# Stick-breaking scores of a head pair: three 64-row matmuls per head on the two halves of the array's rows, in place of two 128-row ones on stacked hi and lo

## The chip, the cores and the metric

The kernel runs on one core of a Trainium2 chip. The metric is the device time of one execution in microseconds (us). The engines are called by the names of the profile: PE is TensorE (matmuls), PEld its weight loads, DVE VectorE, ACT ScalarE, POOL GpSimd, and SP SyncE, whose queue issues nearly all DMAs here.

## What is computed

One decoder layer on a sequence of 1024 tokens of width 1024, in float32: an RMSNorm, one wide input projection, three mixers (an mLSTM, a short convolution, stick-breaking attention), their output projections under sigmoid gates, an MLP and a last RMSNorm. The change concerns the scores `z` of the stick-breaking attention, which has 16 heads of width 64:

```python
def stick_breaking(q, k, v):                      # [1, 1024, 16, 64]
    qf = q.astype(f32) * (d ** -0.5)
    ...
        mask = key_pos[None, :] < q_pos[:, None]
        z = jnp.einsum('bhqd,bshd->bhqs', qblk, kf)
        log_beta = jax.nn.log_sigmoid(z)
        log_1m = jnp.where(mask, log_beta - z, 0.0)
        cum = jnp.cumsum(log_1m, axis=-1)
        log_a = log_beta + cum[..., -1:] - cum
        a = jnp.where(mask, jnp.exp(log_a), 0.0)
        return jnp.einsum('bhqs,bshd->bqhd', a, vf)
```

## The kernel before

**Precision.** Every float32 operand of a matmul is split into a hi part, rounded to the matmul's `fp32r` format, and a lo part, the rest. A product is made of three matmuls, hi x hi, hi x lo and lo x hi, which sum in one PSUM bank (`mm3`, L129 to L132). `split` (L134) makes the parts: ACT copies the hi (L136), DVE subtracts (L137).

**Stages.** The program goes through the mLSTM heads, then the stick-breaking heads, then the three output projections, the output projection and the MLP. The stick-breaking stage lies between 515 and 1245 us. It goes through eight pairs of heads `p`. For each pair, `sb_v` (for every second pair) and `sb_qk` project V, K and Q; `sb_attn` computes the attention; `sc_unit(p)` computes one eighth of the convolution mixer. The projections are dense matmuls of 128 rows and 512 columns (or 256 for V), on lines 130 to 132.

**Scores.** A head has 64 channels and the array 128 rows. `sb_qk` therefore stacks for each head hi and lo: the tile of Q holds its hi in one half of the partitions and its lo in the other; the two tiles of K, `kx` and `ky`, hold (hi, lo) and (lo, hi). The two matmuls of L556 and L557 give (Q hi x K hi + Q lo x K lo) and (Q hi x K lo + Q lo x K hi). To put the hi and lo of K into the other half, `ev_k` sends four DMAs (L530 to L533) per 512 tokens.

**Attention.** `sb_attn` goes through four groups `G` of 256 queries, from the last to the first, then the two heads `hh`, then the two blocks `ti` of 128 queries, then the chunks `ch` of at most 512 keys. For each chunk: two score matmuls into a bank `z` (there are two such banks), two sigmoids on ACT into tiles `u` and `be` (L559, L560), on POOL the mask of the diagonal (L564, L566) or a column handed on (L570), a product scan on DVE (L572), a multiplication on POOL (L573). When a head's four or fewer `be` tiles of the group are done, PE transposes them (L590), ACT and DVE split them, and PE multiplies by V (L603 to L607). There are six `u` and ten `be` tiles.

**Order.** The order of each engine's instructions is set at build time by a scheduler. `sb_attn` is written under `high_priority(offset=AHEAD)`, so that its instructions come first where the scheduler finds them ready; the dense matmuls of the convolution and of the next pair fill the rest of PE's queue. On the chip each queue goes in its fixed order.

Of the kernel before, what the change touches and what calls it, by code (L numbers as in the profile page):

```python
# [11 lines left out]
AF = mybir.ActivationFunctionType  # L12
ALU = mybir.AluOpType
# [3 lines left out]
P = 128  # L17
# [11 lines left out]
C_SBQ, C_SBK, C_SBV = 7176, 8200, 9224  # L29
# [9 lines left out]
def hybrid_block_kernel(  # L39
# [18 lines left out]
    nc = tc.nc  # L58
# [31 lines left out]
    def free(*ts):  # L90
        for t in ts:
            owner[id(t)].free.append(t)
# [13 lines left out]
    def g(name):  # L106
        return rings[name].get()

    def plan(base, **counts):
        for n, c in counts.items():  # L110
            rings[n] = base.carve(n, c)
# [12 lines left out]
    def f32(ap):  # L124
        return ap.bitcast(F32)

    mm = nc.tensor.matmul
# [31 lines left out]
    def dense_ws(w, c0, rhs, evac):  # L159
        parts = load_w(w, 0, KO, c0, P, 4)  # L160
        for th in range(2):
            ps = g("acc")
            for ko in range(KO):
                rh, rl = rhs[ko][th]
                wh, wl = parts[ko // 4]
                ks = slice((ko % 4) * P, (ko % 4 + 1) * P)
                mm3(ps, wh[:, ks], wl[:, ks], rh[:, :512], rl[:, :512], ko == 0, ko == KO - 1)
            evac(th, ps)
            free(ps)
        for p in parts:  # L170
            free(*p)
# [334 lines left out]
        return vt  # L506

    def sb_qk(p):
        Q = [[None, None], [None, None]]
        T = [[None, None] for _ in range(4)]  # L510

        def ev_q(th, ps):
            a, b = g("Q"), g("Q")
            A, B = slice(0, 64), slice(64, 128)
            r = slice(0, 512)
            nc.scalar.activation(a[A, r], ps[A, :], AF.Copy)
            nc.scalar.activation(b[B, r], ps[B, :], AF.Copy)
            nc.vector.tensor_tensor(a[B, r], ps[A, :], f32(a[A, r]), ALU.subtract)
            nc.vector.tensor_tensor(b[A, r], ps[B, :], f32(b[B, r]), ALU.subtract)
            Q[0][th], Q[1][th] = a, b  # L520

        def ev_k(th, ps):
            t1, t2, t3, t4 = [g("T") for i in range(4)]
            A, B = slice(0, 64), slice(64, 128)
            r = slice(0, 512)
            nc.scalar.activation(t1[A, r], ps[A, :], AF.Copy)
            nc.scalar.activation(t2[B, r], ps[B, :], AF.Copy)
            nc.vector.tensor_tensor(t3[A, r], ps[A, :], f32(t1[A, r]), ALU.subtract)
            nc.vector.tensor_tensor(t4[B, r], ps[B, :], f32(t2[B, r]), ALU.subtract)
            nc.sync.dma_start(f32(t1[B, r]), f32(t3[A, r]))  # L530
            nc.sync.dma_start(f32(t3[B, r]), f32(t1[A, r]))
            nc.sync.dma_start(f32(t2[A, r]), f32(t4[B, r]))
            nc.sync.dma_start(f32(t4[A, r]), f32(t2[B, r]))  # L533
            for i, t in enumerate((t1, t2, t3, t4)):
                T[i][th] = t

        dense_ws(w_in, C_SBK + p * P, hT, ev_k)
        dense_ws(w_in, C_SBQ + p * P, hT, ev_q)
        return Q, T

    def sb_attn(p, Q, T, vt):
        for G in range(3, -1, -1):
            yo = g("yo")
            for hh in range(2):
                kx, ky = (T[0], T[2]) if hh == 0 else (T[1], T[3])
                ga = {}
                for ti in (1, 0):
                    Tt = 2 * G + ti
                    qs = Q[hh][Tt // 4][:, (Tt % 4) * P:(Tt % 4 + 1) * P]
                    n = (Tt + 1) * P  # L550
                    nch = (n + 511) // 512
                    prev = None
                    for ch in range(nch - 1, -1, -1):
                        w = min(512, n - ch * 512)
                        ps = g("z")
                        mm(ps[:, :w], qs, kx[ch][:, :w], start=True, stop=False)  # L556
                        mm(ps[:, :w], qs, ky[ch][:, :w], start=False, stop=True)  # L557
                        u, be = g("u"), g("be")
                        nc.scalar.activation(u[:, :w], ps[:, :w], AF.Sigmoid, scale=-0.125)  # L559
                        nc.scalar.activation(be[:, :w], ps[:, :w], AF.Sigmoid, scale=0.125)  # L560
                        free(ps)
                        if prev is None:
                            dg = slice(w - P, w)
                            nc.gpsimd.affine_select(out=u[:, dg], in_=u[:, dg], compare_op=ALU.is_gt, fill=1.0,  # L564
                                                    base=0, pattern=[[-1, P]], channel_multiplier=1)
                            nc.gpsimd.affine_select(out=be[:, dg], in_=be[:, dg], compare_op=ALU.is_gt, fill=0.0,  # L566
                                                    base=0, pattern=[[-1, P]], channel_multiplier=1)
                            nc.gpsimd.memset(u[:, w:w + 1], 1.0)
                        else:
                            nc.gpsimd.tensor_copy(u[:, w:w + 1], prev[:, 0:1])  # L570
                        ur = u[:, 0:w][:, ::-1]
                        nc.vector.tensor_tensor_scan(ur, ur, ur, u[:, w:w + 1], ALU.mult, ALU.bypass)  # L572
                        nc.gpsimd.tensor_tensor(be[:, :w], be[:, :w], u[:, 1:w + 1], ALU.mult)  # L573
                        if prev is not None:
                            free(prev)
                        prev = u
                        ga[ti, ch] = be
                    free(prev)
                pav = g("av")
                ns = 2 * G + 2  # L580
                last = 1 if G else 0
                for s2 in range(G, -1, -1):
                    pt = g("tp")
                    for k in (0, 1):
                        s = 2 * s2 + k
                        for ti in (0, 1):
                            if s == ns - 1 and ti == 0:
                                continue
                            blk = ga[ti, s // 4][:, (s % 4) * P:(s % 4 + 1) * P]
                            nc.tensor.transpose(pt[:, k * 256 + ti * P:k * 256 + (ti + 1) * P], blk, ident)  # L590
                    ah, al = g("ah"), g("ah")
                    if s2 == G:
                        split(ah[:, 0:256], al[:, 0:256], pt[:, 0:256])
                        split(ah[:, 256:384], ah[:, 384:512], pt[:, 384:512])
                    else:
                        split(ah[:, 0:512], al[:, 0:512], pt)
                    free(pt)
                    for k in ((1, 0) if s2 == G else (0, 1)):
                        s = 2 * s2 + k
                        hd = 2 * (p % 2) + hh  # L600
                        vs = vt[s][:, hd * P:(hd + 1) * P]
                        if s == ns - 1:
                            mm(pav[:, 256:512], vs, ah[:, 256:512], start=True, stop=True)  # L603
                            continue
                        o = slice(k * 256, (k + 1) * 256)
                        mm(pav[:, 0:256], vs, ah[:, o], start=(s == ns - 2), stop=False)  # L606
                        mm(pav[:, 0:256], vs, al[:, o], start=False, stop=(s == last))  # L607
                    free(ah, al)
                free(*ga.values())
                tmp = g("avt")  # L610
                hi_r = slice(0, 64) if hh == 0 else slice(64, 128)
                lo_r = slice(64, 128) if hh == 0 else slice(0, 64)
                nc.scalar.activation(tmp[hi_r, 0:512], pav[lo_r, :], AF.Copy)
                nc.vector.tensor_tensor(yo[hi_r, 0:512], pav[hi_r, :], tmp[hi_r, 0:512], ALU.add)
                free(pav, tmp)
            for o in (256, 384):
                nc.vector.tensor_tensor(yo[:, 128:256], yo[:, 128:256], yo[:, o:o + P], ALU.add)
            nc.sync.dma_start(ysb_d[p][:, G * 256:(G + 1) * 256], yo[:, 0:256])
            free(yo)
            if G == 2:  # L620
                free(*[t[1] for t in Q + T])
        free(*[t[0] for t in Q + T])


    def sc_unit(ct):
# [55 lines left out]
            ml_attn(h, st)  # L681
    unplan(ring_r, "q", "k", "v", "ph", "ks", "C")
    unplan(ring_f, "e", "k32", "nmb", "C32", "ft")
    plan(ring_r, Q=6, T=10, V=8, ah=8)
    plan(ring_f, u=6, be=10, yo=2, avt=1)
    vt = None
    for p in range(8):
# [216 lines left out]
    for u in range(FF // 256):  # L904
# [3 lines left out]
        s = {}  # L908
# [130 lines left out]
```

## Time and profile before

| | us |
|---|---|
| median of 3 runs | 2571.91 (2571.35 to 2572.49) |
| the profiled execution | 2567.67 |
| its span, first to last instruction | 2566.0 |
| PE busy in the span | 2510.3 (98%) |
| DVE, ACT, POOL busy | 1323.2, 1036.1, 490.8 |
| PE busy in the stick-breaking stage, 515 to 1245 | 726.57 of 730 |

Times in the rows are counted from the start of the span. A row of the timeline has the start, the duration, the engine, the line, and the operation with its tiles and sizes. `128*128` is the shape of the array's tile that a matmul uses (rows*columns), `128x512` the rows and columns of what it streams. Matmuls are pipelined: a row's duration reaches from its start to its end, and the next row can start earlier. A group of instructions has its count, its busy time in us, the mean duration of one in ns, and the idle time of the engine before them with what ended it.

### The profile page before, as it was taken

Reading aid. Unit: us, or ns where it says so; the run is one execution under the profiler, and the core shown is the slowest. Engines: PE = TensorE matmul, PEld = TensorE weight load, DVE = VectorE, ACT = ScalarE, POOL = GpSimd, SP = SyncE. Lnnn points to the kernel's source line nnn. Section 1 sums busy time; section 2 is a strip of 40 time slices with the busy share of each in tenths; the row PEclk is TensorE's granted clock in tenths of the full one; section 3 lists DMA queues with packets and bytes.
Section 4 is the critical chain, followed back from the end, with each engine's and each line's share of the span. In section 5 each row is a group of like instructions: output and inputs, shape, how many; then the busy total and the mean of one; then the engine's idle time right before and its main releaser. Section 6 shows DMA issues by size and latency. Waiting matters only on the chain.

```text
span 2566.0 us, 34552 instructions
## 1 busy us (share of the span) xinstructions
PE 2510.3 (98%) x12984; PEld 2121.0 (83%) x12984; DVE 1323.2 (52%) x2189; ACT 1036.1 (40%) x2138; POOL 490.8 (19%) x928
## 2 busy tenths in 40 slices
PE   7999999999999999999999999999979999999997
PEld 6899898988888888888888888888858888788886
DVE  6465463767677677577522223224364334444435
ACT  6343333455455455455512212124455555522211
POOL 3000010044344254254100000000263222000000
PEclk9999999999999999999999999999989999999998
DMA  4121111222211221222312313213233334522203
GB/s 121 46 70 46 54 42 54 58 59 58 67 48 51 68 59 44 71 56 60 104 45 74 91 50 99 58 54 123 86 106 109 107 111 139 184 90 83 99 29 111
DMA packets 218560, 197.90 MB, mean 77 GB/s; under 512 B 16400, under 2 KB 176144, under 8 KB 218392
## 3 DMA queue, kind: packets, MB, share of 16 engines
q1 hardware_dynamic: 215944, 191.23, 24.3%
q10 hardware_dynamic: 2448, 4.46, 0.5%
q8 instruction: 102, 1.67, 0.3%
q14 instruction: 66, 0.54, 0.1%
HBM read 149.49 MB, written 37.77 MB: 73 GB/s over the span
## 4 chain that ended last, share of the span: by engine, by line
PE 93%; DVE 3%; DMA 1%; POOL 1%; ACT 1%; issue 1%; SPq 0%; DVEq 0%; POOLq 0%; ACTq 0%
PE ps L130 28%; PE ps L131 28%; PE ps L132 28%; PE ps L590 2%; PE ps L557 1%; PE ps L556 1%; PE ps L607 1%; PE ps L606 1%; DVE gr L137 1%; DVE gf L572 0%; DMA wr<-in_w_in_dram 0%; POOL gf L573 0%; DMA wl<-gd 0%; DMA wr<-in_w_down_dram 0%; DVE gf L1010 0%
## 5 line engine op out<-in xcount | busy, mean ns | idle before, releaser
L132 PE MATMUL ps<-gr,wl 128*128 128x512 f32 x1872 | 740.9, 396 | 2.6 <-DVE wl L137 2.6
L130 PE MATMUL ps<-gr,wh 128*128 128x512 f32 x1856 | 734.6, 396 | 0.0
L131 PE MATMUL ps<-gr,wh 128*128 128x512 f32 x1856 | 734.1, 396 | 0.0
L132 PEld LDWEIGHTS ps<-gr,wl 128*128 128x128 f32 x1872 | 352.1, 188 | 83.9 <-DVE wl L137 3.3
L130 PEld LDWEIGHTS ps<-gr,wh 128*128 128x128 f32 x1856 | 348.9, 188 | 78.7
L131 PEld LDWEIGHTS ps<-gr,wh 128*128 128x128 f32 x1856 | 348.6, 188 | 78.9
L136 ACT ACTIVATE wh<-wr 128x512 fp32r<-128x512 f32 (+1 forms) x268 | 167.7, 631 | 445.7 <-PE ps L131 386.7
L137 DVE TENSOR_TENSOR wl<-wr,wh 128x512 fp32r<-128x512 f32 (+1 forms) x258 | 183.4, 718 | 295.4 <-ACT wh L136 291.0
L132 PE MATMUL ps<-gr,gr 128*128 128x512 f32 (+3 forms) x900 | 330.0, 368 | 1.4 <-DVE gr L137 1.4
L131 PE MATMUL ps<-gr,gr 128*128 128x512 f32 (+3 forms) x900 | 330.7, 369 | 0.0
L130 PE MATMUL ps<-gr,gr 128*128 128x512 f32 (+3 forms) x900 | 327.0, 367 | 1.0 <-ACT gr L136 1.0
L572 DVE TENSOR_TENSOR_SCAN gf<-gf 128x512 f32<-128x512 f32 (+1 forms) x192 | 200.9, 1048 | 100.4 <-POOL gf L564 56.8
L130 PE MATMUL ps<-wh,gr 128*128 128x256 f32 (+2 forms) x800 | 231.1, 290 | 2.6 <-ACT gr L139 2.6
L132 PE MATMUL ps<-wh,gr 128*128 128x256 f32 (+2 forms) x800 | 227.9, 288 | 0.2 <-DVE gr L140 0.2
L131 PE MATMUL ps<-wl,gr 128*128 128x256 f32 (+2 forms) x788 | 224.2, 285 | 0.0
L573 POOL TENSOR_TENSOR gf<-gf,gf 128x512 f32<-128x512 f32 (+1 forms) x192 | 185.3, 967 | 175.8 <-DVE gf L572 144.8
L759 POOL TENSOR_TENSOR gf<-gf,gf 128x512 f32<-128x512 f32 x48 | 68.2, 1426 | 704.5 <-ACT gf L853 575.7
L136 ACT ACTIVATE gr<-ps 128x256 fp32r<-128x256 f32 (+2 forms) x304 | 129.7, 442 | 170.7 <-PE ps L132 70.7
L130 PEld LDWEIGHTS ps<-gr,gr 128*128 128x128 f32 x900 | 169.1, 188 | 32.4 <-ACT gr L136 1.5
L132 PEld LDWEIGHTS ps<-gr,gr 128*128 128x128 f32 x900 | 169.5, 188 | 31.8 <-DVE gr L137 1.9
L131 PEld LDWEIGHTS ps<-gr,gr 128*128 128x128 f32 x900 | 169.4, 188 | 30.2
L137 DVE TENSOR_TENSOR gr<-ps,gr 128x256 fp32r<-128x256 f32 (+2 forms) x304 | 142.7, 483 | 59.1 <-ACT gr L136 56.0
(204 smaller groups left out, 3406.7 us busy)
## 6 DMA issues: line engine op xcount, KB each, us to landing
wr<-in_w_in_dram SPq DMA_DIRECT2D x102, 512.0 KB, 3.7
gd<-gf SPq DMA_DIRECT2D x64, 256.0 KB, 2.7
wr<-in_w_down_dram SPq DMA_DIRECT2D x32, 512.0 KB, 4.0
gr<-gd SPq DMA_DIRECT2D x52, 256.0 KB, 2.8
gf<-in_w_up_dram SPq DMA_DIRECT2D x40, 256.0 KB, 3.0
gr<-gr SPq DMA_DIRECT2D x64, 128.0 KB, 2.2
gf<-in_x_dram SPq DMA_DIRECT2D x31, 256.0 KB, 3.0
wr<-in_w_up_dram SPq DMA_DIRECT2D x24, 256.0 KB, 2.9
```

The costliest lines, as they stand in the source:

```text
L130: mm(ps, lh, rh, start=start, stop=False, skip_group_check=chain)
L131: mm(ps, lh, rl, start=False, stop=False, skip_group_check=chain)
L132: mm(ps, ll, rh, start=False, stop=stop, skip_group_check=chain)
L136: nc.scalar.activation(hi, src, AF.Copy)
L137: nc.vector.tensor_tensor(lo, src, f32(hi), ALU.subtract)
L556: mm(ps[:, :w], qs, kx[ch][:, :w], start=True, stop=False)
L557: mm(ps[:, :w], qs, ky[ch][:, :w], start=False, stop=True)
L572: nc.vector.tensor_tensor_scan(ur, ur, ur, u[:, w:w + 1], ALU.mult, ALU.bypass)
L573: nc.gpsimd.tensor_tensor(be[:, :w], be[:, :w], u[:, 1:w + 1], ALU.mult)
L590: nc.tensor.transpose(pt[:, k * 256 + ti * P:k * 256 + (ti + 1) * P], blk, ident)
L606: mm(pav[:, 0:256], vs, ah[:, o], start=(s == ns - 2), stop=False)
L759: nc.gpsimd.tensor_tensor(dst[:, :512], a[:, :512], b[:, :512], op)
```

## The change

`sb_qk` splits K and Q like every other operand: for 512 tokens one tile with the hi and one with the lo of both heads, head 0 in partitions 0 to 63 and head 1 in 64 to 127. The four DMAs per K eviction fall away. `sb_attn` takes both heads in one pass: for each block and chunk it gets two banks and issues hi x hi, hi x lo and lo x hi, each for head 0 on the upper half of the array's rows and head 1 on the lower half. Then follow the same sigmoids, masks, scans and multiplications for either head. `ga` and `prev` exist for each head; the transposes and the products with V come after both heads' scores of a group. The six Q and ten T tiles become eight and eight.

```diff
     def sb_qk(p):
-        Q = [[None, None], [None, None]]
-        T = [[None, None] for _ in range(4)]
...
-        def ev_k(th, ps):
-            t1, t2, t3, t4 = [g("T") for i in range(4)]
-            A, B = slice(0, 64), slice(64, 128)
-            r = slice(0, 512)
-            nc.scalar.activation(t1[A, r], ps[A, :], AF.Copy)
-            nc.scalar.activation(t2[B, r], ps[B, :], AF.Copy)
-            nc.vector.tensor_tensor(t3[A, r], ps[A, :], f32(t1[A, r]), ALU.subtract)
-            nc.vector.tensor_tensor(t4[B, r], ps[B, :], f32(t2[B, r]), ALU.subtract)
-            nc.sync.dma_start(f32(t1[B, r]), f32(t3[A, r]))
-            nc.sync.dma_start(f32(t3[B, r]), f32(t1[A, r]))
-            nc.sync.dma_start(f32(t2[A, r]), f32(t4[B, r]))
-            nc.sync.dma_start(f32(t4[A, r]), f32(t2[B, r]))
...
+        Q, T = [None, None], [None, None]
+
+        def ev(side, name):
+            def f(th, ps):
+                hi, lo = g(name), g(name)
+                split(hi[:, :512], lo[:, :512], ps)
+                side[th] = (hi, lo)
+            return f
...
     def sb_attn(p, Q, T, vt):
         for G in range(3, -1, -1):
             yo = g("yo")
-            for hh in range(2):
-                kx, ky = (T[0], T[2]) if hh == 0 else (T[1], T[3])
-                ga = {}
-                for ti in (1, 0):
...
-                        ps = g("z")
-                        mm(ps[:, :w], qs, kx[ch][:, :w], start=True, stop=False)
-                        mm(ps[:, :w], qs, ky[ch][:, :w], start=False, stop=True)
...
+            ga = [{}, {}]
+            for ti in (1, 0):
...
+                    pss = [g("z"), g("z")]
+                    qh, ql = Q[Tt // 4]
+                    kh, kl = T[ch]
+                    for m, (l, r) in enumerate(((qh, kh), (qh, kl), (ql, kh))):
+                        for hh in range(2):
+                            hs = slice(hh * 64, hh * 64 + 64)
+                            mm(pss[hh][:, :w], l[hs, qs], r[hs, :w], start=m == 0, stop=m == 2)
+                    for hh in range(2):
+                        ps = pss[hh]
                         u, be = g("u"), g("be")
...
+            for hh in range(2):
                 pav = g("av")
...
-    plan(ring_r, Q=6, T=10, V=8, ah=8)
+    plan(ring_r, Q=8, T=8, V=8, ah=8)
```

The scheduler sets the order anew. In the rows that follow, `ps_166` and `ps_167` are the two score banks (after the change, of head 0 and of head 1), `gr_95` to `gr_110` tiles of Q and K, and lines 130 to 132 dense matmuls; the streamed operand stands first, the loaded one second.

PE, the first scores of the first pair and the second scores after them. Before:

```order
L556 MATMUL ps_166<-gr_105,gr_97 128x512
L557 MATMUL ps_166<-gr_107,gr_97 128x512
L556 MATMUL ps_167<-gr_101,gr_97 128x512
L557 MATMUL ps_167<-gr_103,gr_97 128x512
L130 MATMUL ps_165<-gr_65,wh_154 128x512
```

The same place after the change:

```order
L541 MATMUL ps_166<-gr_105,gr_97 128x512
L541 MATMUL ps_167<-gr_105,gr_97 128x512
L541 MATMUL ps_166<-gr_106,gr_97 128x512
L541 MATMUL ps_167<-gr_106,gr_97 128x512
L541 MATMUL ps_166<-gr_105,gr_98 128x512
L541 MATMUL ps_167<-gr_105,gr_98 128x512
L130 MATMUL ps_165<-gr_65,wh_154 128x512
```

Here the two heads alternate. PE again, after the change, the next two chunks, some 20 dense matmuls further on:

```order
L131 MATMUL ps_165<-gr_94,wh_155 128x512
L541 MATMUL ps_166<-gr_103,gr_97 128x512
L541 MATMUL ps_166<-gr_104,gr_97 128x512
L541 MATMUL ps_166<-gr_103,gr_98 128x512
L132 MATMUL ps_165<-gr_93,wl_160 128x512
L130 MATMUL ps_164<-gr_63,wh_156 128x512
L541 MATMUL ps_167<-gr_103,gr_97 128x512
L541 MATMUL ps_167<-gr_104,gr_97 128x512
L541 MATMUL ps_167<-gr_103,gr_98 128x512
L131 MATMUL ps_164<-gr_64,wh_156 128x512
```

Here the scheduler has put each head's three together, with dense matmuls between the heads. Of the 576 score matmuls after the change, most stand as in this second piece; the score matmuls form 185 unbroken runs, where there were 188 before.

## Rows read from the trace of the kernel before

**Rows 1.** The page: busy us (share of the span) and instructions of each engine.

```profile
PE 2510.3 (98%) x12984; PEld 2121.0 (83%) x12984; DVE 1323.2 (52%) x2189; ACT 1036.1 (40%) x2138; POOL 490.8 (19%) x928
```

**Rows 2.** Busy us by stretch (PE, PEld, DVE, ACT, POOL, granted clock), and the stage's sum.

```profile
515.00:606.00 91.00, 91.00 (x468) 76.66 (x467) 64.37 (x93) 49.19 (x104) 39.13 (x82) 1.00 0.23 62
...
sum 730.00, PE 726.57 PEld 625.41 DVE 518.73 ACT 393.51 POOL 309.94; mean PE 90.82 PEld 78.18 DVE 64.84 ACT 49.19 POOL 38.74
```

**Rows 3.** What PE waited for, 515 to 1245 us: us, times, longest us.

```profile
PE ps L607 <- DVE gr L137: 2.9, 3, 1.0
PE ps L603 <- DVE gr L137: 0.2, 1, 0.2
```

**Rows 4.** Timeline, matmuls and weight loads: start us, us, what.

```profile
527.62 0.39 PE L131 MATMUL ps<-gr,wh 128*128 128x512 f32 x1
...
529.48 0.39 PE L556 MATMUL ps<-gr,gr 128*128 128x512 f32 x1
529.48 0.19 PEld L557 LDWEIGHTS ps<-gr,gr 128*128 128x128 f32 x1
...
529.71 0.40 PE L557 MATMUL ps<-gr,gr 128*128 128x512 f32 x1
...
535.54 0.40 PE L131 MATMUL ps<-gr,wh 128*128 128x512 f32 x1
```

**Rows 5.** The two score lines: count, ns min/median/max, first and last start, forms.

```profile
L556 PE MATMUL ps<-gr,gr x192: 218/388/483, 529.5 to 1232.1; 128*128 128x512 f32 x96, 128*128 128x384 f32 x32, 128*128 128x256 f32 x32, 128*128 128x128 f32 x32
L557 PE MATMUL ps<-gr,gr x192: 270/389/486, 529.7 to 1232.2; 128*128 128x512 f32 x96, 128*128 128x384 f32 x32, 128*128 128x256 f32 x32, 128*128 128x128 f32 x32
```

**Rows 6.** Timeline of PE: score matmuls of 384, 256 and 128 columns.

```profile
535.78 0.34 PE L556 MATMUL ps<-gr,gr 128*128 128x384 f32 x1
535.95 0.34 PE L557 MATMUL ps<-gr,gr 128*128 128x384 f32 x1
536.13 0.39 PE L132 MATMUL ps<-gr,wl 128*128 128x512 f32 x1
...
659.79 0.28 PE L556 MATMUL ps<-gr,gr 128*128 128x256 f32 x1
659.91 0.28 PE L557 MATMUL ps<-gr,gr 128*128 128x256 f32 x1
660.02 0.28 PE L130 MATMUL ps<-wh,gr 128*128 128x256 f32 x1
...
662.16 0.22 PE L556 MATMUL ps<-gr,gr 128*128 128x128 f32 x1
662.22 0.27 PE L557 MATMUL ps<-gr,gr 128*128 128x128 f32 x1
662.33 0.33 PE L132 MATMUL ps<-wh,gr 128*128 128x256 f32 x1
662.50 0.28 PE L130 MATMUL ps<-wh,gr 128*128 128x256 f32 x1
```

**Rows 7.** DMA issues: count, KB each, median us from issue to landing.

```profile
gr<-gr SPq DMA_DIRECT2D x64, 128.0 KB, 2.2
```

**Rows 8.** Groups by line: a half's copy on ACT, a half's subtraction on DVE.

```profile
L517 ACT ACTIVATE gr<-ps 64x512 fp32r<-64x512 f32 x16 | 9.5, 593 | 0.2
...
L529 DVE TENSOR_TENSOR gr<-ps,gr 64x512 fp32r<-64x512 f32 x15 | 10.4, 695 | 1.9 <-PE ps L556 1.6
```

**Rows 9.** Timeline of PE: two gate transposes with another tile shape among 264-column matmuls.

```profile
28.45 0.28 PE L131 MATMUL ps<-wl,gr 128*128 128x264 f32 x1
28.57 0.27 PE L282 MATMUL ps<-ident,gcol 128*4 128x128 f32 x1
28.68 0.27 PE L283 MATMUL ps<-ident,gcol 128*4 128x128 f32 x1
28.70 0.37 PE L130 MATMUL ps<-wh,gr 128*128 128x264 f32 x1
28.91 0.29 PE L131 MATMUL ps<-wl,gr 128*128 128x264 f32 x1
```

More of the change, by code (lines that the diff above doesn't have):

```diff
@@ L508, in sb_qk @@
     def sb_qk(p):
-        Q = [[None, None], [None, None]]
-        T = [[None, None] for _ in range(4)]
-        def ev_q(th, ps):
-            a, b = g("Q"), g("Q")
-            A, B = slice(0, 64), slice(64, 128)
-            r = slice(0, 512)
[L516 to L520, printed above, removed]
-        def ev_k(th, ps):
-            t1, t2, t3, t4 = [g("T") for i in range(4)]
-            A, B = slice(0, 64), slice(64, 128)
-            r = slice(0, 512)
-            nc.scalar.activation(t1[A, r], ps[A, :], AF.Copy)
-            nc.scalar.activation(t2[B, r], ps[B, :], AF.Copy)
-            nc.vector.tensor_tensor(t3[A, r], ps[A, :], f32(t1[A, r]), ALU.subtract)
-            nc.vector.tensor_tensor(t4[B, r], ps[B, :], f32(t2[B, r]), ALU.subtract)
-            nc.sync.dma_start(f32(t1[B, r]), f32(t3[A, r]))
-            nc.sync.dma_start(f32(t3[B, r]), f32(t1[A, r]))
-            nc.sync.dma_start(f32(t2[A, r]), f32(t4[B, r]))
-            nc.sync.dma_start(f32(t4[A, r]), f32(t2[B, r]))
[L534 to L538, printed above, removed]
+        Q, T = [None, None], [None, None]
[5 more added lines that the diff above has]
+            return f
+        dense_ws(w_in, C_SBK + p * P, hT, ev(T, "T"))
+        dense_ws(w_in, C_SBQ + p * P, hT, ev(Q, "Q"))
         return Q, T
@@ L543, in sb_attn @@
             yo = g("yo")
-            for hh in range(2):
-                kx, ky = (T[0], T[2]) if hh == 0 else (T[1], T[3])
-                ga = {}
-                for ti in (1, 0):
[L548 to L554, printed above, removed]
-                        ps = g("z")
-                        mm(ps[:, :w], qs, kx[ch][:, :w], start=True, stop=False)
-                        mm(ps[:, :w], qs, ky[ch][:, :w], start=False, stop=True)
+            ga = [{}, {}]
+            for ti in (1, 0):
+                Tt = 2 * G + ti
+                qs = slice((Tt % 4) * P, (Tt % 4 + 1) * P)
+                n = (Tt + 1) * P
+                nch = (n + 511) // 512
+                prev = [None, None]
+                for ch in range(nch - 1, -1, -1):
+                    w = min(512, n - ch * 512)
+                    pss = [g("z"), g("z")]
[7 more added lines that the diff above has]
+                        ps = pss[hh]
                         u, be = g("u"), g("be")
@@ L561, in sb_attn @@
                         free(ps)
-                        if prev is None:
+                        if prev[hh] is None:
                             dg = slice(w - P, w)
@@ L569, in sb_attn @@
                         else:
-                            nc.gpsimd.tensor_copy(u[:, w:w + 1], prev[:, 0:1])
+                            nc.gpsimd.tensor_copy(u[:, w:w + 1], prev[hh][:, 0:1])
                         ur = u[:, 0:w][:, ::-1]
@@ L573, in sb_attn @@
                         nc.gpsimd.tensor_tensor(be[:, :w], be[:, :w], u[:, 1:w + 1], ALU.mult)
[L574 to L578, printed above, removed]
+                        if prev[hh] is not None:
+                            free(prev[hh])
+                        prev[hh] = u
+                        ga[hh][ti, ch] = be
+                free(*prev)
+            for hh in range(2):
                 pav = g("av")
@@ L588, in sb_attn @@
                                 continue
-                            blk = ga[ti, s // 4][:, (s % 4) * P:(s % 4 + 1) * P]
+                            blk = ga[hh][ti, s // 4][:, (s % 4) * P:(s % 4 + 1) * P]
                             nc.tensor.transpose(pt[:, k * 256 + ti * P:k * 256 + (ti + 1) * P], blk, ident)
@@ L608, in sb_attn @@
                     free(ah, al)
-                free(*ga.values())
+                free(*ga[hh].values())
                 tmp = g("avt")
@@ L620, in sb_attn @@
             if G == 2:
-                free(*[t[1] for t in Q + T])
-        free(*[t[0] for t in Q + T])
+                free(*Q[1], *T[1])
+        free(*Q[0], *T[0])
     def sc_unit(ct):
```

## The prediction

> **What bounds the kernel now.** I read the page's busy table first, then busy time by stretch, then what TensorE waits for, then the matmuls one by one. The profiled execution took 2567.67 us, 1.65 of them outside its span, and TensorE is busy for 98% of that span [rows 1]. An average says little about one stage, so the next view is the attention stage alone, from 515 to 1245 us, cut into eight stretches of about one head pair: TensorE is busy 726.57 of 730 us there, at a granted clock of 1.00, the upper of the two levels (2.4 GHz) [rows 2]. The next engine, DVE, has 518.73. What TensorE waited for in the stage adds up to 3.1 us, nearly all of it three waits for a split on DVE [rows 3]. As busy matmuls overlap in this trace, busy time alone could mislead; the starts settle it. From 527.62 to 535.78 there are 35 matmuls of 512 columns, one each 8.16 / 35 = 0.233 us, score matmuls (L556, L557) among dense ones without a hole [rows 4]. So TensorE's queue is the path in this stage, and it has filler: whenever attention is not ready, dense matmuls of the next projections stand in the queue. A matmul more in this queue costs its spacing, one fewer gives it back, and what happens on other engines counts only if TensorE comes to wait for it.
>
> **The scores: what they cost now.** There are 96, 32, 32 and 32 matmuls of 512, 384, 256 and 128 columns on each of the two lines [rows 5]. Their price is the distance to the next start, not their duration of 0.39 us. It is 0.233 us for 512 columns [rows 4], 0.175 for 384 (535.78, 535.95, 536.13), 0.117 for 256 (659.79, 659.91, 660.02), and for 128 columns 0.11: L556 (662.16), L557 and a 256-column matmul take until the next start at 662.50, and 0.34 - 0.117 leaves 0.22 for the two [rows 6]. Hence 192 x 0.233 + 64 x 0.175 + 64 x 0.117 + 64 x 0.11 = 44.7 + 11.2 + 7.5 + 7.0 = 70.4 us.
>
> **What is added.** Three matmuls of the same width and the same 128 loaded columns stand where two stood: 576 for 384. If a 64-row matmul takes its turn like a 128-row one, the scores cost 70.4 x 1.5 = 105.6 us, which is **+35.2 us**. The number of columns streamed sets the spacing, and half of the rows lying idle doesn't shorten it: in rows 4 and 6 the spacing follows the columns (0.233 and 0.117 for 512 and 256).
>
> **What can be given back.** Two matmuls on opposite halves may run side by side, but only where they are neighbours in TensorE's queue. The diff writes six matmuls alternating between the heads; the built order does not keep that. Of its 185 unbroken runs of score matmuls, 127 are three of one head, 26 one or two of one head, and only 32 hold both: at 512 columns 8 runs of six, 4 of five, 4 of four and 4 of two, all alternating; four alternating runs of six at 128 columns; and eight in which one head's matmul merely abuts the other's. No row of this trace shows two matmuls side by side, so the price has two ends. One end is nothing. The other is full overlap, in which the alternating 512-column runs save 8 x 3 + 4 x 2 + 4 x 2 + 4 x 1 = 44 spacings of 0.233, 10.3 us, and the others at most 4 x 3 x 0.11 + 4 x 0.117 + 4 x 0.11 = 2.2: 12.5 us in all. Between them lies the weight load. Each matmul has its own; it starts as the matmul before it starts [rows 4], and 128-column matmuls, which leave nothing but the load to wait for, come no closer than 0.11 us [rows 6]. With starts 0.11 apart and 0.233 on the same half, an alternating six ends after 0.809 us instead of 1.398 and saves 0.589; five save 0.466, four 0.356, two 0.123; 128-column runs save nothing, and the four pairs of 384 and 256 columns 0.065 each. That is 4.7 + 1.9 + 1.4 + 0.5 + 0.3 = **-8.8 us**. I take this value, because a load and a matmul do run beside one another in rows 4 and the halves have separate weights and banks, while nothing there shows two loads at once. Added and given back: +35.2 - 8.8 = **+26.4 us**.
>
> The Trainium skill bears on this on its page TensorE: Matmul & The Clock Gate, Part 3, Packing small matmuls: matmuls that target different row groups run concurrently, about 4 ns apart at their starts, and only matmuls that follow each other do, since they start and end in program order. By its figure the sum would be the full-overlap end, an estimate of +22.7; no row here shows it.
>
> **What is removed and moved.** Each K eviction loses four SBUF-to-SBUF DMAs, 64 in all of 128 KB and 2.2 us [rows 7], and each K or Q eviction becomes one 128-partition ACT and one DVE instruction in place of two of 64 partitions (some 593 and 695 ns each [rows 8]). On ACT and DVE that is 32 instructions fewer, some 19 us each. All of it is costed at nothing, because TensorE hardly waits: no score matmul waited for a K copy, dense matmuls stood ahead of it, and rows 3 name no DMA. The gain can't exceed the stage's waits of 3.1 us. The SP queue only loses work; its weight loads move up and were not late. The loops now hold both heads' weights of a group: up to 8 of the 10 `be` tiles instead of 4, and both score banks at once. Where a group then has to wait for the group before, dense matmuls stand behind it in the same queue and wait too. The built order puts such matmuls ahead (23 dense ones between the first two score runs), so I put nothing in the sum, from -3.1 to the bound of the third rival.
>
> **The switch of tile shape** is the large unknown. Now 185 runs of 64-row matmuls lie between 128-row ones: 370 switches. The nearest rows are the gate transposes, which use a tile of 128 rows and few columns, among 264-column matmuls: the switch in comes 0.12 us after a 264-column start, as any other; the second transpose and the 264-column matmul behind it take from 28.68 to 28.91, 0.23, which is just 0.11 + 0.12 [rows 9]. Nothing was lost. The other bound is that the array empties first: a matmul lasts 0.39 us [rows 4] and the next starts after 0.23, so 0.16 would be exposed, 370 x 0.16 = 59 us. I take zero, since rows 9 are an actual change of shape; they split columns and not rows, so the other end stays in the range.
>
> **The rivals.**
> 1. The halves don't run side by side (the change doesn't do what its loop says): +35.2, **2607 us**. For it: no pair is seen beside another in the trace. Against it: load and matmul already are.
> 2. Every switch empties the array: +26.4 + 59 = **2657 us**, and 2608 to 2657 for a part of it. Against it: rows 9. The Trainium skill speaks for it on its page TensorEngine Tiling (Array Packing), Key Properties: changing the tiling mode drains the engine. The trace doesn't agree for the column tile of rows 9, and says nothing of a row tile.
> 3. A new wait: the 32 groups (8 pairs of 4) each hold up the queue for the longest wait seen now, 1.0 us [rows 3]: +26.4 + 32 = **2630 us**. Against it: the filler.
> 4. Faster. TensorE lets the second head's three matmuls pass over the dense ones between and run beside the first head's: then 576 matmuls cost as 288, 52.8 us, -17.6, **2554 us**. It decides from 35.2 / 0.233 = 151 side-by-side 512-column pairs on; the order has 44 as neighbours. For it: weight loads run ahead of matmuls. Against it: the matmuls of rows 4 and 6 start in program order.
>
> **How the numbers follow.** The sum is a difference, so it is added to the median of 2571.91, which lies 4.2 us above the profiled execution: 2571.9 + 26.4 = **2598 us**. The forecast has 0.38 (its own range 2591 to 2604, from full overlap and the waits gone to half the overlap); rival 1 has 0.19, rival 2 0.25, rival 3 0.06, rival 4 0.06, and 0.06 goes to a mixture that ends within 0.2%, 5 us, which is about what a measurement of this kernel can tell from no change. The range 2588 to 2640 leaves out rival 4, the no-change case and the upper third of rival 2, 0.08: 2 in 10. Faster 0.06, same 0.06, slower 0.88.
>
> **What would show it.** In the profile after, 576 score matmuls with a tile of 64 rows; the stage some 26 us longer, at the same busy share; where A B A B stand in a row, starts 0.11 and 0.12 apart by turns; where three of one head stand, 0.233. Starts 0.233 apart in the alternating runs mean rival 1; an extra gap before and behind each run rival 2; named waits of TensorE for ACT, DVE or POOL in the stage rival 3. A stage that isn't longer would prove the forecast wrong outright.

## The result, and the profile after

The changed kernel takes 2660.89 us (median of 5 runs, 2658.59 to 2661.34) against 2572.49 us before: 88.4 us more, a ratio of 1.034 (95% interval 1.0324 to 1.0355). The forecast was 2598 with a range up to 2640; rival 2 stood at 2657.

The page's first lines after, busy time and instructions, answer to [rows 1]:

```profile
span 2659.2 us, 34649 instructions
PE 2602.5 (98%) x13176; PEld 2132.0 (80%) x13176; DVE 1317.9 (50%) x2157; ACT 1020.2 (38%) x2106; POOL 509.5 (19%) x928
```

TensorE's share is 98% as before, and its 93 us more of span are 92 us more of busy time. Busy time by stretch, the stage now being some 89 us longer, and what PE waited for in it (to [rows 2, 3]):

```profile
515.00:1334.00 819.00, 817.67 (x4241) 636.14 (x4240) 511.87 (x761) 378.01 (x834) 331.50 (x651) 1.00 0.14 41
...
PE ps L590 <- DVE gr L137: 1.3, 3, 0.4
```

No new wait is named, the granted clock is 1.00, and PE counts as busy for 817.67 of 819 us. Read by its busy share this stage looks perfect. Yet the matmuls don't explain it: 192 more cost 35.2 us at most, and 89 came. The time is inside what counts as busy, between the starts. Here is the timeline at the first scores of the first pair, matmuls (PE) and weight loads (PEld), and at the next scores after them:

```profile
528.87 0.19 PEld L132 LDWEIGHTS ps<-gr,wl 128*128 128x128 f32 x1
529.10 0.40 PE L132 MATMUL ps<-gr,wl 128*128 128x512 f32 x1
529.42 0.53 PEld L541 LDWEIGHTS ps<-gr,gr 64*128 64x128 f32 x6 [0.36 <-issue]
529.42 0.96 PE L541 MATMUL ps<-gr,gr 64*128 64x512 f32 x6
...
530.31 0.19 PEld L130 LDWEIGHTS ps<-gr,wh 128*128 128x128 f32 x1 [0.36 <-issue]
530.32 0.50 PE L130 MATMUL ps<-gr,wh 128*128 128x512 f32 x1
530.42 0.19 PEld L131 LDWEIGHTS ps<-gr,wh 128*128 128x128 f32 x1
530.65 0.40 PE L131 MATMUL ps<-gr,wh 128*128 128x512 f32 x1
...
535.56 0.40 PE L131 MATMUL ps<-gr,wh 128*128 128x512 f32 x1
535.88 0.53 PEld L541 LDWEIGHTS ps<-gr,gr 64*128 64x128 f32 x3 [0.37 <-issue]
535.89 0.96 PE L541 MATMUL ps<-gr,gr 64*128 64x512 f32 x3
...
536.77 0.50 PE L132 MATMUL ps<-gr,wl 128*128 128x512 f32 x1
...
537.11 0.40 PE L130 MATMUL ps<-gr,wh 128*128 128x512 f32 x1
```

Two things are to be seen. First, **six alternating matmuls take the time of three of one head**: 0.90 us from 529.42 to the next start at 530.32, and 0.88 from 535.89 to 536.77. Their loads also took the same 0.53. The halves do run side by side, loads and all. Second, **a price at each switch**. In [rows 4] the load for the next matmul starts together with the matmul before it. Here it doesn't: the last dense matmul starts at 529.10, the first 64-row load at 529.42, 0.32 later, which is 0.09 after the 0.233 that the columns take. Only then the load runs, which takes 0.11 (from 530.31, one load, to 530.42, the next), and as far as the rows show no column flows meanwhile: the matmul that starts with the load (530.32) lasts 0.50 in place of 0.40, and the next one starts 0.33 after it in place of 0.233. The loads' row has the gap as 0.36 us of idle time ended by `issue`, which means that nothing the profile can name was waited for. On the way into the 64-row tile and on the way back the same happens. From 529.10 to 530.65 it takes 1.55 us; a dense matmul, three steps of pairs and another dense one are 5 x 0.233 = 1.165. The rest is 0.385 us for two switches, **0.19 us each**. From 535.56 to 537.11 the numbers are the same.

Over all 185 runs, from where the columns before have ended to where the load behind is done, the starts add up to 164.8 us; with the pairs side by side the matmuls alone would take 105.6 - 12.5 = 93.1. That leaves 71.7 us for 370 switches, 0.194 each, whatever the columns before or behind (medians of 0.19 to 0.20 us for 512, 384, 256 and 128).

The rule of the Trainium skill that speaks of this, in TensorEngine Tiling (Array Packing), Key Properties, gives no price: changing the mode drains the engine. This trace agrees for the tile of 64 rows, 0.09 us to the load, and adds that the load behind it, 0.11, is exposed as well. With 64 of the 128 columns in use e4_before_64cols, below, shows no drain; whether that changes the mode at all, no run shows.

### The profile page after: what moved, and what is told of

Same layout as the page of the kernel before. It is cut to its first block, busy times and chain, and to the rows that moved or that the text cites. A ratio compares the mean times of both kernels' runs of the same rounds, so it can differ in the third digit from the quotient of the medians.

```text
span 2659.2 us, 34649 instructions
## 1 busy us (share of the span) xinstructions
PE 2602.5 (98%) x13176; PEld 2132.0 (80%) x13176; DVE 1317.9 (50%) x2157; ACT 1020.2 (38%) x2106; POOL 509.5 (19%) x928
## 4 chain that ended last, share of the span: by engine, by line
PE 96%; DVE 2%; DMA 1%; ACT 1%; issue 0%; SPq 0%; POOL 0%; DVEq 0%
PE ps L130 28%; PE ps L131 28%; PE ps L132 28%; PE ps L541 5%; PE ps L577 2%; PE ps L593 1%; PE ps L594 1%; DVE gr L137 1%; PE ps L590 0%; DMA wr<-in_w_down_dram 0%; DVE gf L997 0%; PE ps L838 0%; PE ps L456 0%; DMA gf<-in_x_dram 0%; DMA wl<-gd 0%
## 5 line engine op out<-in xcount | busy, mean ns | idle before, releaser
L558 DVE TENSOR_TENSOR_SCAN gf<-gf 128x512 f32<-128x512 f32 (+3 forms) x192 | 219.0, 1145 | 111.3 <-POOL gf L550 87.2
L559 POOL TENSOR_TENSOR gf<-gf,gf 128x512 f32<-128x512 f32 (+3 forms) x192 | 190.1, 995 | 158.9 <-DVE gf L558 128.8
L136 ACT ACTIVATE gr<-ps 128x512 fp32r<-128x512 f32 (+2 forms) x336 | 148.2, 456 | 177.1 <-PE ps L132 102.4
L137 DVE TENSOR_TENSOR gr<-ps,gr 128x512 fp32r<-128x512 f32 (+2 forms) x336 | 164.1, 503 | 103.3 <-ACT gr L136 101.3
```

What stands on the lines that cost most here:

```text
L136: nc.scalar.activation(hi, src, AF.Copy)
L137: nc.vector.tensor_tensor(lo, src, f32(hi), ALU.subtract)
```

## The experiments

Theory A: each change of the tile's row shape costs 0.2 us, and opposite halves run side by side. Theory B, the main rival: the new loops and their order bring waits, which hold up the queue.

**e1_full_rows: the changed kernel without the switch.**

```diff
-   mm(pss[hh][:, :w], l[hs, qs], r[hs, :w], start=m == 0, stop=m == 2)
+   mm(pss[hh][:, :w], l[:, qs], r[:, :w], start=m == 0, stop=m == 2)
```

> The changed kernel with every score matmul on all 128 rows (each head's scores then sum over both heads' channels, which is not what is wanted). The order in every queue is that of the changed kernel, 185 runs of score matmuls; only the tile's shape is gone, and with it the halves side by side. Theory A, each change of the tile's row shape costs 0.2 us and halves run side by side: the 370 switches (74 us) go, 12.5 us of side-by-side work come back: 2660.9 - 74 + 12.5 = 2599, which is 27 us above the kernel before. Theory B, the new order and its waits (both score banks taken at once, both heads' tiles held for a group) cost the time: no change from 2661 but for the 12.5 us, 2661 to 2673.

Measured: 2603.35 us against 2571.9 before on the same chip, +31.4 (ratio 1.012, 1.0103 to 1.0137). The same order of instructions without 64-row tiles is 57.5 us faster, though it gives up what runs side by side. Theory B falls: loops, banks and tiles are those of the changed kernel. What is left is the price of 192 matmuls more, 35.2 in the sum, 31.4 here (26.5 to 35.2 by the interval). The timeline of PE at the first scores; six matmuls now take 1.39 us:

```profile
529.63 0.39 PE L132 MATMUL ps<-gr,wl 128*128 128x512 f32 x1
529.87 1.56 PE L541 MATMUL ps<-gr,gr 128*128 128x512 f32 x6
531.26 0.40 PE L130 MATMUL ps<-gr,wh 128*128 128x512 f32 x1
531.49 0.39 PE L131 MATMUL ps<-gr,wh 128*128 128x512 f32 x1
```

**e2_before_64rows: the kernel before with the switch alone.**

```diff
-   mm(ps[:, :w], qs, kx[ch][:, :w], start=True, stop=False)
-   mm(ps[:, :w], qs, ky[ch][:, :w], start=False, stop=True)
+   mm(ps[:, :w], qs[0:64, :], kx[ch][0:64, :w], start=True, stop=False)
+   mm(ps[:, :w], qs[0:64, :], ky[ch][0:64, :w], start=False, stop=True)
```

> The kernel before, with its two score matmuls per head on rows 0 to 63 only (of the scores only one of the two products in each matmul is kept). Same count of matmuls, same loops, no side-by-side pairs; the score matmuls now form 196 runs with another tile shape, 392 switches. Theory A: 2572.5 + 392 x 0.2 = 2651. Theory B: 2572, since neither the loops nor the count changed.

Measured: 2643.53 us, +71.6 (ratio 1.0281, 1.0266 to 1.0296), 0.183 us for each of 392 switches. Not a matmul more, the old loops, and half the rows at work: this is the disputed cost by itself. PE's timeline:

```profile
529.25 0.40 PE L132 MATMUL ps<-gr,wl 128*128 128x512 f32 x1
529.58 0.50 PE L556 MATMUL ps<-gr,gr 64*128 64x512 f32 x1
529.91 0.39 PE L557 MATMUL ps<-gr,gr 64*128 64x512 f32 x1
530.15 0.39 PE L556 MATMUL ps<-gr,gr 64*128 64x512 f32 x1
530.38 0.39 PE L557 MATMUL ps<-gr,gr 64*128 64x512 f32 x1
530.70 0.50 PE L130 MATMUL ps<-gr,wh 128*128 128x512 f32 x1
531.04 0.39 PE L131 MATMUL ps<-gr,wh 128*128 128x512 f32 x1
```

The first 64-row matmul starts 0.33 after the dense one, its successor 0.33 later instead of 0.233, and so again at 530.70 and 531.04; between them the steps are 0.23.

**e3_before_96rows: fewer rows, but more than half.** The edit is that of e2_before_64rows with 96 for 64.

> The kernel before, with its score matmuls on rows 0 to 95 (part of the lo products is left out). 96 rows still use the tile of 128 rows, so the count of active rows changes and the tile's shape doesn't; 188 runs. Theory A (it is the tile's shape): 2572, no change. Rival A2 (any change of the active rows empties the array): 2572.5 + 376 x 0.2 = 2648.

Measured: 2572.45 against 2571.9, ratio 1.0001 (0.9992 to 1.0011). Fewer rows alone don't bring the price. The profile writes `96*128`, which is the count of rows and columns in use, and the matmul goes through like one of 128 rows:

```profile
529.06 0.39 PE L132 MATMUL ps<-gr,wl 128*128 128x512 f32 x1
529.29 0.40 PE L556 MATMUL ps<-gr,gr 96*128 96x512 f32 x1
529.53 0.40 PE L557 MATMUL ps<-gr,gr 96*128 96x512 f32 x1
```

**e4_before_64cols: fewer columns in use.**

```diff
-   mm(ps[:, :w], qs, kx[ch][:, :w], start=True, stop=False)
-   mm(ps[:, :w], qs, ky[ch][:, :w], start=False, stop=True)
+   mm(ps[0:64, :w], qs[:, 0:64], kx[ch][:, :w], start=True, stop=False)
+   mm(ps[0:64, :w], qs[:, 0:64], ky[ch][:, :w], start=False, stop=True)
```

(The two score banks are set to zero once, ahead of the stage.)

> The kernel before, with its score matmuls loading 64 columns only (the scores of 64 of every 128 queries are left out). The tile is 128 rows by 64 columns, so its shape changes by columns instead of rows; 191 runs. If only a change of the row shape empties the array, as the gate transposes in the trace before suggest: 2572, no change. If every change of shape does: 2572.5 + 382 x 0.19 = 2645.

Measured: 2566.22 against 2571.07, ratio 0.9984 (0.9974 to 0.9993): no price, even 4.9 us less. PE's timeline shows the steps of 0.23 on the way in and on the way out:

```profile
529.67 0.39 PE L132 MATMUL ps<-gr,wl 128*128 128x512 f32 x1
529.90 0.39 PE L556 MATMUL ps<-gr,gr 128*64 128x512 f32 x1
530.13 0.39 PE L557 MATMUL ps<-gr,gr 128*64 128x512 f32 x1
530.36 0.39 PE L556 MATMUL ps<-gr,gr 128*64 128x512 f32 x1
530.58 0.40 PE L557 MATMUL ps<-gr,gr 128*64 128x512 f32 x1
530.82 0.40 PE L130 MATMUL ps<-gr,wh 128*128 128x512 f32 x1
```

What [rows 9] showed was true, then, but of the loaded columns only. Nor is it shown that anything switches here: `128*64`, like `96*128` above, says how many rows and columns are in use, and no run tells whether the array changes its mode for it. Where two matmuls with 128 streamed columns stand together, the two take 0.16 us here instead of 0.22 (with the delay of the next), as their loads are half as wide; by the starts that is some 1.8 of the 4.9 us, and the rest stays open.

**e7_one_half: the switches without anything side by side.**

```diff
-   hs = slice(hh * 64, hh * 64 + 64)
+   hs = slice(0, 64)
```

> The changed kernel with both heads' score matmuls on the upper half (head 1 gets head 0's scores). Same order, same 370 switches, nothing side by side. Theory A: 2660.9 + 12.5 = 2673. If the halves didn't run side by side in the changed kernel: 2661.

Measured: 2673.02 us (ratio 1.0396, 1.038 to 1.0411, to the kernel before), +12.1 on the changed kernel; full overlap in the 24 alternating and 8 abutting runs was worked out at 12.5. The alternating six take 1.59 us here (529.58 to 531.17), where they took 0.90:

```profile
529.25 0.40 PE L132 MATMUL ps<-gr,wl 128*128 128x512 f32 x1
529.58 1.67 PE L541 MATMUL ps<-gr,gr 64*128 64x512 f32 x6
531.17 0.50 PE L130 MATMUL ps<-gr,wh 128*128 128x512 f32 x1
531.51 0.40 PE L131 MATMUL ps<-gr,wh 128*128 128x512 f32 x1
```

**e5_six_together: fewer switches and more pairs.** Edges for the scheduler keep a chunk's six matmuls in one row and let the first start only when both banks are free.

```diff
...
+   if last_mm is not None:
+       after(i, last_mm)
+   else:
+       for rd in z_read:
+           after(i, rd, mybir.DependencyClass.Sync)
+   last_mm = i
...
```

> The changed kernel with one edge more for the scheduler, which makes the six matmuls of a chunk start when both banks are free: 113 runs in place of 185, nearly all alternating. Theory A: all pairs side by side make the scores 70.4 x 0.75 = 52.8 us, -17.6 against before; 226 switches cost 226 x 0.19 = 43: 2572.5 - 17.6 + 43 = 2598. Theory B (the waits for both banks cost the time): more than 2661, as the wait is now for both banks by force.

Measured: 2603.0 us against 2571.07, +31.9 (ratio 1.0127, 1.0112 to 1.0142), 5 us above theory A's sum and 58 below the changed kernel. What PE waited for in the stage is 8.4 us in five rows, where it was 1.3; the largest:

```profile
PE ps L603 <- DVE gr L137: 3.4, 3, 1.6
PE ps L590 <- POOL gf L565: 1.9, 1, 1.9
PE ps L130 <- DVE gr L137: 1.5, 3, 0.5
```

So the two terms scale as the theory says. None of the five rows is a score matmul waiting for a bank, so holding out for both banks costs at most a few us, not tens.

**e6_four_banks and e8_four_banks_128rows: still fewer switches.** Two chunks of both heads stand in one run, in a pool of four banks that the products with V share; e8 has the same grouping with the old stacked matmuls of 128 rows.

```diff
+   if G >= 2:
+       batches = [[(ti, 1), (ti, 0)] for ti in (1, 0)]
+   else:
+       batches = [[(1, 0), (0, 0)]]
...
-   pav = g("av")
+   pav = g("z")
...
+   unplan(banks, "z", "av")
+   plan(banks, z=4)
```

> The changed kernel with two chunks of both heads in one run of twelve: the banks of the scores and of the products with V are one pool of four. 40 runs, 80 switches, all pairs side by side. Theory A: 2572.5 - 17.6 + 80 x 0.19 = 2570, level with before, 2566 to 2572. Theory B: above 2661.

> The same runs and the same four banks with the two 128-row matmuls on stacked hi and lo of the kernel before: 40 runs of eight, no change of the tile's shape, the K copies by DMA as before. It tells what the new grouping alone does. Theory A: 2572, no change, as the count and price of matmuls are those of before; if the grouping saves waits, down to 2564; if it brings waits, above 2575.

Measured: 2859.66 us (ratio 1.113, 1.1111 to 1.1148) and 2892.48 us (1.1254, 1.1236 to 1.1273). Both expectations missed by far. I had priced the matmuls and the switches and left out what the grouping does to the queue. Busy time by stretch of e6 (PE first, the granted clock after POOL), and what PE waited for:

```profile
900.00:1300.00 400.00, 291.42 (x1594) 244.38 (x1593) 208.89 (x300) 145.57 (x332) 146.90 (x256) 0.80 0.09 28
...
960.00:965.00 5.00, 0.42 (x2) 0.43 (x3) 2.30 (x4) 1.73 (x4) 5.00 (x12) 0.50 0.01 2
...
PE ps L598 <- POOL gf L580: 111.4, 22, 8.7
PE ps L611 <- DVE gr L137: 34.8, 22, 3.2
PE ps L548 <- ACT gf L567: 22.0, 8, 2.9
```

The transposes (L598) now wait for POOL's multiplications, up to 8.7 us at a time, and with PE idle for over a quarter of the stretch the granted clock was 0.80 in the mean; from 960 to 965 us, with PE busy for 0.42 of 5 us, it was 0.50, the lower of the two levels (1.2 GHz). That is rival 3 in a kernel in which it does decide. The 64 rows aren't needed for it, as e8 is slower still.

**e9_four_score_banks and e10_four_score_banks_128rows: the same, with banks apart.** The four banks are the scores' alone; the products with V take a bank of the transposes (`pav = g("tp")`).

> As the kernel with runs of twelve, but the four banks are the scores' alone, and the products with V take a bank of the transposes: the built order has 60 runs of score matmuls, 120 switches, all pairs side by side. If the shared pool was what held TensorE up there: 2572.5 - 17.6 + 120 x 0.194 = 2578. If holding two chunks of both heads back is enough to starve the queue: above 2661.

> The same grouping and banks with the two 128-row matmuls on stacked hi and lo of the kernel before, and so no switch: 2572 if the grouping costs nothing. Its distance to the 64-row kernel of the same grouping is then the price of the 64-row scores in few runs: by theory A, -17.6 + 23.3 = +6 us.

Measured: 2972.21 (ratio 1.1555, 1.1538 to 1.1572) and 2998.58 us (1.1653, 1.1634 to 1.1672). The banks apart don't help. Whether the shared pool held e6_four_banks up isn't shown by this, since taking a bank from the transposes makes a new wait: they now wait for the sum that frees the bank of the products:

```profile
PE ps L598 <- DVE gf L622: 129.9, 43, 5.7
PE ps L611 <- DVE gr L137: 78.2, 46, 4.0
```

In both grouped pairs the 64-row form is the faster one, by 33 and 26 us, where theory A had it 6 us slower with the banks apart, but as PE isn't the bound there, this is no measure of the matmuls. No run here beats the kernel before with its full computation.

**e11_two_full_rows: what is left of the change without its matmuls.** e1_full_rows with the third product left out:

```diff
-   for m, (l, r) in enumerate(((qh, kh), (qh, kl), (ql, kh))):
+   for m, (l, r) in enumerate(((qh, kh), (qh, kl))):
...
-   mm(pss[hh][:, :w], l[:, qs], r[:, :w], start=m == 0, stop=m == 2)
+   mm(pss[hh][:, :w], l[:, qs], r[:, :w], start=m == 0, stop=m == 1)
```

> The changed kernel's evictions, loops and tiles with two 128-row score matmuls per head in place of three 64-row ones (the product of Q's lo part is left out, and the scores sum over both heads). The count, the shape and the price of the matmuls are those of the kernel before; what remains of the change is the K and Q evictions in halves the instructions, 64 DMAs fewer and both heads in one pass. If that is worth nothing, as predicted: 2571.5. If it is where the some 4 us come from by which the 128-row form of the changed kernel stayed under its sum: 2567 to 2568.

Measured: 2577.53 against 2570.28 us, +7.3 (ratio 1.0025, 1.0015 to 1.0035), above both expectations. Half the eviction instructions of K and Q and 64 DMAs fewer bring nothing that can be seen; in the scheduler's other order the stage has waits of 8.3 us, where [rows 3] had 3.1:

```profile
PE ps L590 <- DVE gr L137: 6.3, 3, 2.1
PE ps L130 <- DVE gf L601: 2.0, 1, 2.0
```

## Why the prediction was wrong

**What bounds the kernel: right.** What was added to TensorE's queue came out in the run nearly whole, and the rest didn't matter: e1_full_rows changed the matmuls and moved the time; the evictions and DMAs of e11_two_full_rows didn't give any back. (Two slips had no weight: the 32 instructions fewer on DVE are 32 x 0.695 = 22 us, not 19, and 1.7 us of the profiled execution lay outside its span, not 1.65.)

**What is added: right, perhaps a little high.** +35.2 in the sum; e1_full_rows measured +31.4 with the same count, order and columns, and its interval ends at 35.2.

**What can be given back: right in kind, too small.** I took 8.8 us, because weight loads would come one after another. Loads on opposite halves run side by side as well, so that six take the time of three: 12.5 worked out, 12.1 measured by e7_one_half. In the trace the two of a pair start some 3 ns apart, and not 0.11 us. My bound of 0.11 was misread, too: in [rows 6] two starts are 0.06 apart (662.16, 662.22), and 0.11 is what such a matmul costs with the delay of the next. That matmuls on different parts of the array run at the same time is what Part 3 (Packing small matmuls) in TensorE: Matmul & The Clock Gate of the Trainium skill states; the runs agree, with 0.90 us for six against 0.88 for three. The count of runs from the built order was right, and it mattered: with only 44 pairs of 512 columns side by side, this term could never have paid for the added one.

**The switch of tile shape: the step that failed.** I set it to zero by [rows 9], in which a tile of 128 rows and few columns stands between 128-row matmuls at no cost. That nothing was lost there was read rightly, and e4_before_64cols confirms it for 191 runs. But I called these rows an actual change of shape because of the profile's `128*4`, and that is only the count of rows and columns in use: in e3_before_96rows `96*128` costs nothing either. They change the columns, perhaps without any switch of the array, and the change made here is one of rows. That one e2_before_64rows prices by itself, 0.183 us each; in the changed kernel the 370 cost 71.7 us, 0.194 each, where the sum had nothing. The sentence that kept the other end in the range had noticed that rows are not columns; the chance of 0.38 for zero against 0.25 for rival 2 had not. The bound was also too low. I let the array empty (0.16) and forgot that a load, which is otherwise hidden under the matmul before, then can't be: the trace has 0.09 of emptying and 0.11 of load. Two terms that I had in front of me in [rows 4] and [rows 6] give an upper bound that holds, 0.16 + 0.11 = 0.27 us a switch.

**Rival 2 had the right step, an extra gap before and behind each run, but its 2657 us came within 4 us of the result by luck, by two errors that cancel** (0.16 for 0.194 a switch, 8.8 for 12.5 given back) and a remainder.

**The remainder.** +35.2 - 12.5 + 71.7 = 94.4, and 88.4 were measured. These 6 us are no more than what executions of the kernel before differ by over all runs (2567.67 to 2575.48); between the two profiled executions the span grew by 93 us (2566.0 to 2659.2), 89 of them in the stage. e1_full_rows came out 3.8 below its sum already without a switch, at the edge of its interval. The waits that fell away in the stage (3.1 to 1.3 us) are at most 1.8. e11_two_full_rows gives no sign that the evictions did it, since its time went up. The rest stays open.

**Rival 3, a new wait: did not happen** in the changed kernel (1.3 us of waits in the stage), nor with the six kept together (8.4). It did in the four grouped kernels, which were 290 to 430 us slower in all, waits and lower clock together. **Rival 4** had no ground: matmuls started in program order throughout.

## What to carry to other kernels

Price a matmul on half the rows by its runs, not by its count: each stretch of 64-row matmuls between 128-row ones costs about 0.4 us here, as much as 1.7 matmuls of 512 columns, while each side-by-side pair gives back one. Look in the built order for how long the runs are before counting on the halves, since a scheduler may put other work between them. And where the nearest row of a trace shows the same kind of event on another axis, it is evidence for that axis alone, and a shape that the profile prints is no evidence that anything switched; a bound must then include every step that the event could expose, the hidden weight load too.

## What the runs showed of the hardware

- Changing the tile between 128 and 64 rows costs 0.19 to 0.20 us each way, for 512 to 128 columns alike: the next load starts some 0.09 us after the last columns, and its 0.11 us are not hidden.
- Loading 64 or 4 columns in place of 128, at 128 rows, costs nothing on the way in or out (e4_before_64cols, ratio 0.9984, and [rows 9]), and 96 rows go like 128 (ratio 1.0001). Whether fewer columns change the array's mode is not shown.
- 64-row matmuls on opposite halves run side by side in full, with their loads: 0.90 us for six of 512 columns, 0.88 for three of one half, 1.59 for six on one half (e7_one_half).
- None of this lowers the busy share of TensorE: it was 98% before and after, and no wait is named. The distance between starts shows it, and the 0.36 us of idle time that the weight loads have at each switch.
